# A hybrid decoder layer on one core: 32 more tokens take the gathered-rows path of the expert stage, 352 dense token columns instead of 384

## The chip, the cores and the metric

The kernel runs on one core of a Trainium2 chip. The metric is the device time of one execution in microseconds (us), lower is better. TensorE (PE) multiplies, VectorE (DVE) and ScalarE (ACT) work elementwise, GpSimd (POOL) issues the indirect DMAs, SyncE (SP) issues most other DMAs. 16 DMA engines serve all queues.

## What is computed

One decoder layer of 512 tokens with 2048 features in float32: two token mixers, a merge with a residual, an expert stage (PEER), a gated per-layer input and a last norm. The change touches the expert stage alone. It is, cut to what matters:

```python
q = (hf @ wq).reshape(N, PEER_HEADS, 2, half)            # 8 heads
s1 = jnp.einsum('nhc,kc->nhk', q[:, :, 0], k1)           # 128 keys per half
s2 = jnp.einsum('nhc,kc->nhk', q[:, :, 1], k2)
v1, i1 = lax.top_k(s1, 16); v2, i2 = lax.top_k(s2, 16)
cand = (v1[..., :, None] + v2[..., None, :]).reshape(N, PEER_HEADS, 256)
cv, ci = lax.top_k(cand, 16)
e_idx = i1[ci // 16] * 128 + i2[ci % 16]                 # one of 16384 experts
gate = softmax(cv)
z = einsum('thkd,td->thk', u_tab[e_idx], h)              # 128 slots per token
out = einsum('thk,thkd->td', gelu(z) * gate, v_tab[e_idx])
```

Each token has 128 slots (8 heads of 16 experts). A slot costs a dot product with a row of `u_tab` and an addition of a scaled row of `v_tab`, rows of 2048 float32 (8 KB).

## The kernel before

The features lie on the partitions and the tokens along the free axis, except where rows are gathered. Every float32 weight is used as a high and a low float32r part: `Stream.split` makes the high part on ACT (L111) and the low part on DVE (L112), and `mm3` (L147 to L149) does three matmuls per pair of tiles. The weights come through rings: four raw halves of 512 KB, four high and four low halves. `Ahead.step` loads two blocks ahead and splits one block ahead.

The 512 tokens of the expert stage are in two groups.

- **Group A**, the first 128 tokens (`NA`), takes the gathered-rows path. Its tokens are on the partitions. For slot s one indirect DMA (L779, on POOL's queue) fetches 128 rows of 8 KB, 1 MB together, one row for each token. `dot_u` multiplies them with the tokens' own rows `hrow` and sums (L785, DVE, 128x2048), for 128 slots. In the second half the same is done with `peer_v`: `axpy_v` adds each row times its coefficient to `outA` (L1083, DVE, 128x2048). There are two row buffers: each `dot_u` or `axpy_v` ends with the gather into the buffer that it has just read, so the gather for slot s+2 waits for the dot of slot s.
- **Group B**, the other 384 tokens (`NB`), takes the dense path: all 16384 experts. The loop over `j` (`NU` = 128 steps, "the U loop") multiplies 128 experts of `u` with the 384 columns `hBh`, `hBl`: 16 tiles of features times three matmuls, 48 matmuls of 384 columns a step. The result goes through Gelu to DRAM (`z_s`, L984 and L985). The gate matrix [i1, i2, token] is made by `gate_tokens`, four tokens (a quad) at a time: four one-hot rows on DVE (L833) and ACT (L832, L838), four matmuls of 256 columns (L843), and a copy and an addition into `stage` (L848 on ACT, L849 on DVE), which goes to `G_s` in DRAM. The loop over groups of eight blocks and 8 pairs of output tiles (`NV` = 120 steps, "the V loop", and 8 last steps) loads `z_s` and `G_s` again, multiplies them (L1003), splits (L154, L155), does 48 matmuls of 384 columns a step and adds the result up (L1091).

The order is written by hand (`manual_schedule`): an engine executes its instructions in the order in which the code emits them. In a step of the U loop stand on DVE: the two low parts of the next block, the additions into `stage` that were left over, then a share of a list `work` (the top-k of the three blocks of group B and the quads, each with a cost, 16 steps for the first block's top-k, 2 times 36 steps for top-k and quads together, 22 steps for the last quads), and then the dots. The dots are spread evenly over 120 steps (from step 7 on): 128 dots are one a step, and two in every 15th step. In a step of the V loop stand on DVE: two low parts, the second addition of the step before (L1091), the product of gate and activation (L1003), the axpys, spread over the 120 steps like the dots, the low part of the activation (L155), and the first addition (L1091), which waits for PE.

Two lines set the pace of dots and axpys:

```python
while dots and 129 - len(dots) <= 128 * n / (NU - 1 - NF) + 1e-9:     # U loop, NF = 7
while axpys and 129 - len(axpys) <= 128 * (n + 1) / NV + 1e-9:        # V loop
```

Of the kernel before, what the change touches and what calls it, by code (L numbers as in the profile page):

```python
# [10 lines left out]
F32 = mybir.dt.float32  # L11
F32R = mybir.dt.float32r
# [8 lines left out]
T = 512  # L21
D = 2048
KT = 16
NA = 128
NB = T - NA
NJ = 8
# [20 lines left out]
def kernel(ctx: ExitStack, tc: tile.TileContext, a, dbg=None):  # L47
# [14 lines left out]
    # ---------------------------------------------------------------- helpers  # L62
# [14 lines left out]
    class Ring:  # L77
        """Buffers taken in turn."""
# [42 lines left out]
    class Ahead:  # L121
        """Streams of a list of blocks: loaded two steps ahead, split one step ahead."""
# [28 lines left out]
    def split(hi, lo, src, gain=None):  # L151
        """hi + lo = src * gain, both float32r."""
# [29 lines left out]
    def rstd_cols(ss, n, name):  # L182
        """[128 tokens, blocks] of 1/sqrt(ss/n + eps)."""
# [13 lines left out]
    def sums_over_features(sq):  # L197
        """[128 tokens, 4] PSUM sums over the partitions of sq [128, T]."""
# [6 lines left out]
    def rows_of(rc, out=None):  # L205
        """[128, tokens], in out or else in PSUM: every partition holds the row of rc."""
# [11 lines left out]
    class SumSq:  # L218
        """Sum of squares of [128, T] chunks over features."""
# [18 lines left out]
    # ---------------------------------------------------------------- constants  # L238
# [21 lines left out]
    # ---------------------------------------------------------------- DRAM scratch  # L260
# [39 lines left out]
    # ---------------------------------------------------------------- HGRN2  # L300
# [147 lines left out]
    # ---------------------------------------------------------------- gates (kept before the sigmoid)  # L448
# [6 lines left out]
    # ---------------------------------------------------------------- MLA  # L455
# [17 lines left out]
    # rotary tables: angle = position * frequency, reduced to [-pi, pi]  # L473
# [49 lines left out]
    for hp in range(4):  # L523
# [21 lines left out]
        # a head's rotary part: its 64 rows of high parts, and in the other 64 rows their low parts  # L545
# [58 lines left out]
    # ---------------------------------------------------------------- merge  # L604
# [35 lines left out]
    # ---------------------------------------------------------------- residual, second norm  # L640
# [20 lines left out]
    hBl = hpool.tile([128, 16, NB], F32R, name="hBl")  # L661
    hrow = hpool.tile([128, D], F32, name="hrow")
# [38 lines left out]
    def topk(b, i1o, i2o, gate):  # L701
        """Steps (cost, function) that fill i1o, i2o, gate: [128 tokens, 8 heads * 16] float32."""
# [57 lines left out]
    # ---- group A: expert rows gathered for the first 128 tokens  # L760
    def prep_A():
# [3 lines left out]
        def experts():  # L765
            V.scalar_tensor_tensor(i1, i1, 128.0, i2, op0=OP.mult, op1=OP.add)
            V.tensor_copy(eA, i1)
            gather(a["peer_u"], 0)
            gather(a["peer_u"], 1)
# [5 lines left out]
    in_flight = {}  # L775

    def gather(tab, s):
        row = rows()
        G.indirect_dma_start(out=row, out_offset=None, in_=tab,  # L779
                             in_offset=bass.IndirectOffsetOnAxis(ap=eA[:, s:s + 1], axis=0))  # L780
        in_flight[s] = row

    def dot_u(s):
        row = in_flight.pop(s)
        V.scalar_tensor_tensor(row, row, 1.0, hrow, op0=OP.mult, op1=OP.mult,  # L785
                               accum_out=zA[:, s:s + 1])
        if s + 2 < 128:
            gather(a["peer_u"], s + 2)
        else:
            gather(a["peer_v"], s + 2 - 128)  # L790

    # ---- group B: the gate matrix [i1, i2, token]
# [3 lines left out]
    def prep_B(b):  # L796
        i1 = upool.tile([128, 128], F32, name="i1", bufs=2)
        i2 = upool.tile([128, 128], F32, name="i2", bufs=2)
        gt = upool.tile([128, 128], F32, name="gt", bufs=1)

# [16 lines left out]
        return topk(b + 1, i1, i2, gt) + [(0, turn)]  # L817
# [3 lines left out]
    def gate_tokens(t0):  # L821
        """Gate matrices of tokens t0 .. t0+3 of group B."""
# [35 lines left out]
    def merge(*lists):  # L858
        """The lists' steps in one list, each list spread evenly over it."""
# [10 lines left out]
    # ---------------------------------------------------------------- PEER scores  # L870
# [38 lines left out]
    def rows_of_h(c):  # L909
        """Group A's h by rows, 512 of its columns."""  # L910
# [7 lines left out]
        S.activation(hrow[:, c * 512:(c + 1) * 512], ps, AF.Copy)  # L918

    pending = None  # L920
    for cg in range(4):
# [28 lines left out]
        if cg == 0:  # L950
# [4 lines left out]
            zA = gpool.tile([128, 128], F32, name="zA")  # L955
            rows = Ring(gpool, 2, [128, D], F32, "row")
# [5 lines left out]
            # the top-k steps of group A that need the heads of a column group only  # L962
# [10 lines left out]
    hApool.release()  # L973

# [5 lines left out]
    dots = list(range(128))  # L980

    def finish(z, j):
        zg = t2()[:, :NB]
# [26 lines left out]
    for j in range(NU):  # L1010
# [6 lines left out]
        if j >= NF:  # L1017
# [14 lines left out]
        if j == 1:  # L1032
            scores_mul(3, pending)
        todo = after_pe + after_pe_next
# [6 lines left out]
        if j == NU - 7:  # L1041
# [6 lines left out]
            zts = Ring(vwA, 2, [128, 4, NB], F32, "zt")  # L1048
            gts = Ring(vwA, 2, [128, NB // TC, 4, TC], F32, "gt")
            vwB = tc.alloc_tile_pool(name="vwB", bufs=1, side="left")  # L1050
            ahs = Ring(vwB, NJ, [128, NB], F32R, "ah")
            als = Ring(vwB, NJ, [128, NB], F32R, "al")
# [9 lines left out]
    dump("zA", zA)  # L1062
    hpool.release()
# [3 lines left out]
    outA = V_.tile([128, D], F32, name="outA")  # L1067
# [308 lines left out]
```

## Time and profile before

| | |
|---|---|
| median of 3 runs | 4041.68 us (4041.59 to 4042.62) |
| span of the profiled execution, first to last instruction | 4040.0 us |
| PE busy | 4005.3 us, 99% |
| DVE busy | 2621.1 us, 65% |
| ACT busy | 1597.2 us, 40% |
| U loop, 128 steps | about 1643 to 2771 us of the span |
| V loop, 120 steps and 8 last ones | about 2771 to 3836 us |
| clock granted to PE | full in every stage but the last |

The page gives no other time of the profiled execution than its span; the median of the runs is 1.7 us longer. Busy times are averages over stages with different limits, so the section of rows below takes the stages one by one. Matmuls are pipelined, so the time that one costs is read from the distance of the starts of its neighbours, not from its duration. The same holds for DVE's instructions: each row's duration reaches a little into the next one's.

### The profile page before, as it was taken

The numbers are of one execution on the slowest core, as the hardware profiler recorded it, in microseconds if no ns is written. First come the engines' busy times: TensorE is split into PE (matmuls) and PEld (weight loads), VectorE is DVE, ScalarE is ACT, GpSimd is POOL, SyncE is SP. The second block draws the span as 40 slices with busy tenths as digits, with TensorE's granted clock in tenths as the row PEclk, the third lists the DMA queues.
The fourth block names the chain that finished last, engine by engine and source line by source line (L and its number), as shares of the span: only waits on it lengthen the run. The fifth ranks groups of instructions, "written<-read, shape, count | busy, mean of one in ns | idle before, by whom it ended". The sixth has DMA issues, their size and how long they took to land. (4 is left out here: it accounts for less than half of the span.)

```text
span 4040.0 us, 54629 instructions
## 1 busy us (share of the span) xinstructions
PE 4005.3 (99%) x21191; PEld 3667.2 (91%) x21191; DVE 2621.1 (65%) x3992; ACT 1597.2 (40%) x2582; POOL 347.6 (9%) x262
## 2 busy tenths in 40 slices
PE   9999999999999999999999999999999999999998
PEld 7878777778888889999999999999999999999976
DVE  5352554443343343699998998977777888877744
ACT  5342433332332242325566555753333333333443
POOL 0000000000000000021221211111111111111000
PEclk9999999999999999999999999999999999999999
DMA  5222222334444442478787788789888888888432
GB/s 210 97 74 94 72 96 84 102 105 141 151 141 133 141 140 99 166 286 304 283 303 283 287 302 298 293 332 356 317 297 315 312 311 312 299 313 310 169 117 97
DMA packets 264515, 862.68 MB, mean 214 GB/s; under 512 B 24128, under 2 KB 94272, under 8 KB 229568
## 3 DMA queue, kind: packets, MB, share of 16 engines
q1 hardware_dynamic: 202064, 531.57, 38.5%
q0 software_dynamic: 36864, 268.45, 17.8%
q10 hardware_dynamic: 25328, 59.17, 3.8%
q8 instruction: 168, 2.75, 0.3%
q14 instruction: 91, 0.75, 0.1%
HBM read 780.44 MB, written 78.64 MB: 213 GB/s over the span
## 5 line engine op out<-in xcount | busy, mean ns | idle before, releaser
L111 ACT ACTIVATE hi<-raw 128x1024 fp32r<-128x1024 f32 x806 | 851.4, 1059 | 1606.9 <-PE acc L148 1371.9
L112 DVE TENSOR_TENSOR lo<-raw,hi 128x1024 fp32r<-128x1024 f32 x806 | 975.0, 1221 | 782.6 <-ACT hi L111 779.5
L147 PE MATMUL acc<-hBh,hi 128*128 128x384 f32 x2304 | 775.0, 336 | 0.0
L148 PE MATMUL acc<-hBl,hi 128*128 128x384 f32 x2304 | 774.5, 336 | 0.0
L149 PE MATMUL acc<-hBh,lo 128*128 128x384 f32 x2304 | 774.4, 336 | 0.0
L148 PEld LDWEIGHTS acc<-hBl,hi 128*128 128x128 f32 x2304 | 433.1, 188 | 3.0 <-DVE hBl L155 0.2
L147 PEld LDWEIGHTS acc<-hBh,hi 128*128 128x128 f32 x2304 | 433.1, 188 | 2.7
L149 PEld LDWEIGHTS acc<-hBh,lo 128*128 128x128 f32 x2304 | 433.1, 188 | 0.0
L779 POOL DMA_INDIRECT row<-in_peer_u_dram,eA x128 | 198.9, 1554 | 2551.1 <-DMA raw<-in_uT_dram 1703.2
L149 PE MATMUL acc<-xh,lo 128*128 128x512 f32 x912 | 363.9, 399 | 0.0
L147 PE MATMUL acc<-xh,hi 128*128 128x512 f32 x912 | 363.4, 398 | 0.0
L148 PE MATMUL acc<-xl,hi 128*128 128x512 f32 x912 | 362.6, 398 | 0.0
L147 PE MATMUL acc<-ahx,hi 128*128 128x384 f32 x1024 | 344.7, 337 | 0.0
L148 PE MATMUL acc<-alx,hi 128*128 128x384 f32 x1024 | 344.1, 336 | 0.0
L149 PE MATMUL acc<-ahx,lo 128*128 128x384 f32 x1024 | 344.1, 336 | 0.0
L147 PE MATMUL acc<-ah,hi 128*128 128x384 f32 x1024 | 344.1, 336 | 0.0
L148 PE MATMUL acc<-al,hi 128*128 128x384 f32 x1024 | 344.1, 336 | 0.0
L149 PE MATMUL acc<-ah,lo 128*128 128x384 f32 x1024 | 344.1, 336 | 0.0
L1083 DVE SCALAR_TENSOR_TENSOR outA<-row,coef,outA 128x2048 f32<-128x2048 f32 x127 | 298.0, 2346 | 16.6 <-DMA row<-in_peer_v_dram,eA 16.3
L785 DVE SCALAR_TENSOR_TENSOR row<-row,hrow 128x2048 f32<-128x2048 f32 x128 | 292.0, 2283 | 20.5 <-DMA row<-in_peer_u_dram,eA 20.4
L779 POOL DMA_INDIRECT row<-in_peer_v_dram,eA x128 | 147.5, 1152 | 860.3 <-DVE outA L1083 799.6
L149 PEld LDWEIGHTS acc<-xh,lo 128*128 128x128 f32 x912 | 171.4, 188 | 43.0 <-issue 2.4
(379 smaller groups left out, 6270.5 us busy)
## 6 DMA issues: line engine op xcount, KB each, us to landing
raw<-in_uT_dram SPq DMA_DIRECT2D x256, 512.0 KB, 6.9
raw<-in_vB_dram SPq DMA_DIRECT2D x256, 512.0 KB, 5.7
z_s<-t ACTq DMA_DIRECT2D x128, 192.0 KB, 4.9
G_s<-stage ACTq DMA_DIRECT2D x12, 2048.0 KB, 14.4
zt<-z_s SPq DMA_DIRECT2D x32, 768.0 KB, 7.4
gt<-G_s SPq DMA_DIRECT2D x32, 768.0 KB, 12.1
raw<-in_w_ga_dram SPq DMA_DIRECT2D x32, 512.0 KB, 3.5
raw<-in_w_gb_dram SPq DMA_DIRECT2D x32, 512.0 KB, 3.5
```

The costliest lines, as they stand in the source:

```text
L111: S.activation(hi, raw, AF.Copy)
L112: V.tensor_tensor(lo, raw, hi.bitcast(F32), op=OP.subtract)
L147: TE.matmul(out, lhsT=lh, rhs=rh, start=start, stop=False)
L148: TE.matmul(out, lhsT=lh, rhs=rl, start=False, stop=False)
L149: TE.matmul(out, lhsT=ll, rhs=rh, start=False, stop=stop)
L779: G.indirect_dma_start(out=row, out_offset=None, in_=tab, in_offset=bass.IndirectOffsetOnAxis(ap=eA[:, s:s + 1], axis=0))
L785: V.scalar_tensor_tensor(row, row, 1.0, hrow, op0=OP.mult, op1=OP.mult, accum_out=zA[:, s:s + 1])
L1083: V.scalar_tensor_tensor(outA, row, coef[:, s:s + 1], outA, op0=OP.mult, op1=OP.add)
```

## The change

32 tokens (`NX`, the last of group B) leave the dense path. `ND` = 352 columns remain in it. The 32 tokens, called X, take the gathered-rows path: with four copies of each token on the 128 partitions, partition r*32+t holds part r of token t's slots, so 32 gathers of 1 MB (and not 128) hold its 128 slots. `dot_u` and `axpy_v` run over 160 row sets in place of 128, in the same number of steps: one, one, two, and so on. The U rows of X come last, the V rows of X first. New are `rows_of_hX` (X's rows, four copies, in U steps 2 to 5), `experts_X` (indices and gates moved to the four parts), an accumulator `outX`, and in the last 8 steps two more transposes each and the sum of the four parts. The top-k of the third block of group B, which holds X, is now made first, and its quads, 24 instead of 32, come first too. The projection that makes the scores still has 384 columns.

```diff
+NX = 32
+RX = 128 // NX
 NB = T - NA
+ND = NB - NX
...
-    z_s = dram.tile([128 // NJ, 128, NJ, NB], F32, name="z_s")
-    G_s = dram.tile([NB // TC, 128, 128 * TC], F32, name="G_s")
+    z_s = dram.tile([128 // NJ, 128, NJ, ND], F32, name="z_s")
+    G_s = dram.tile([ND // TC, 128, 128 * TC], F32, name="G_s")
...
+    hBd = [(hBh[:, k, :ND], hBl[:, k, :ND]) for k in range(16)]
...
-    in_flight = {}
...
-    def dot_u(s):
-        row = in_flight.pop(s)
-        V.scalar_tensor_tensor(row, row, 1.0, hrow, op0=OP.mult, op1=OP.mult,
-                               accum_out=zA[:, s:s + 1])
...
+    in_flight = []
+    order = [(a["peer_u"], 0, s) for s in range(128)] + [(a["peer_u"], 1, s) for s in range(NX)]
+    order += [(a["peer_v"], 1, s) for s in range(NX)] + [(a["peer_v"], 0, s) for s in range(128)]
...
+    def dot_u():
+        row, x, s = in_flight.pop(0)
+        z = zX if x else zA
+        V.scalar_tensor_tensor(row, row, 1.0, hrowX if x else hrow, op0=OP.mult, op1=OP.mult,
+                               accum_out=z[:, s:s + 1])
+        gather()
...
+        def experts_X():
+            e, x = t2()[:, :128], slice(128 - NX, 128)
+            V.scalar_tensor_tensor(e[x], i1[x], 128.0, i2[x], op0=OP.mult, op1=OP.add)
+            for r in range(RX):
+                V.tensor_copy(eX[r * NX:(r + 1) * NX], e[x, r * NX:(r + 1) * NX])
+                S.activation(gateX[r * NX:(r + 1) * NX], gt[x, r * NX:(r + 1) * NX], AF.Copy)
...
-    quads = [[(2, lambda t=t: gate_tokens(t)) for t in range(b * 128, (b + 1) * 128, 4)] for b in range(3)]
+    quads = [[(2, lambda t=t: gate_tokens(t)) for t in range(b * 128, min((b + 1) * 128, ND), 4)] for b in range(3)]
...
-            work = phase(B0, prep_B(0))
-            for b in (1, 2):
-                prep = prep_B(b)
-                work += phase(MIX, merge(prep[:-1], quads[b - 1]) + prep[-1:])
-            work += phase(NW - NF - B0 - 2 * MIX, quads[2])
+            work = phase(B0, prep_B(2))
+            for b, b1 in ((2, 0), (0, 1)):
+                prep = prep_B(b1)
+                work += phase(MIX, merge(prep[:-1], quads[b]) + prep[-1:])
+            work += phase(NW - NF - B0 - 2 * MIX, quads[1])
...
-            while dots and 129 - len(dots) <= 128 * n / (NU - 1 - NF) + 1e-9:
-                dot_u(dots.pop(0))
-        z = acc()[:, :NB]
+            while dots and NDOT + 1 - dots <= NDOT * n / (NU - 1 - NF) + 1e-9:
+                dots -= 1
+                dot_u()
+        z = acc()[:, :ND]
         for k in range(KT):
-            mm3(z, *cur.part(k, KT), hBh[:, k], hBl[:, k], k == 0, k == KT - 1)
+            mm3(z, *cur.part(k, KT), *hBd[k], k == 0, k == KT - 1)
...
+        if 2 <= j < 6:
+            rows_of_hX(j - 2)
...
-            while axpys and 129 - len(axpys) <= 128 * (n + 1) / NV + 1e-9:
-                axpy_v(axpys.pop(0))
+            while axpys and NDOT + 1 - axpys <= NDOT * (n + 1) / NV + 1e-9:
+                axpys -= 1
+                axpy_v()
...
+            V.tensor_reduce(sX[h], oT[:, h * 256 + 128:h * 256 + 256].rearrange("p (r t) -> p t r", r=RX),
+                            axis=AX.X, op=OP.add)
+            V.tensor_tensor(x2[:, d, NA + ND:], x2[:, d, NA + ND:], sX[h], op=OP.add)
```

How the order changes is shown at two places. The first is DVE in the U loop, late in the stretch of top-k and quads. `row` is a row buffer, `lo` the low part of a weight block, `ohr` a quad's one-hot rows, `stage` the gate matrix, `zA` the dots' results; the rows of the scratch tile `t` (L738 to L741, after the change L742 to L745) look up indices. Before:

```order
L785 SCALAR_TENSOR_TENSOR row_9654,zA<-row_9654,hrow 128x2048
L112 TENSOR_TENSOR lo_80<-raw_72,hi_76 128x1024
L112 TENSOR_TENSOR lo_81<-raw_73,hi_77 128x1024
L833 SCALAR_TENSOR_TENSOR ohr<-cst,slots 128x256 x8
L785 SCALAR_TENSOR_TENSOR row_9653,zA<-row_9653,hrow 128x2048
L112 TENSOR_TENSOR lo_82<-raw_74,hi_78 128x1024
L112 TENSOR_TENSOR lo_83<-raw_75,hi_79 128x1024
```

And after the change, at a step with two dots:

```order
L796 SCALAR_TENSOR_TENSOR row_9657,zA<-row_9657,hrow 128x2048
L115 TENSOR_TENSOR lo_80<-raw_72,hi_76 128x1024
L115 TENSOR_TENSOR lo_81<-raw_73,hi_77 128x1024
L848 SCALAR_TENSOR_TENSOR ohr<-cst,slots 128x256 x8
L796 SCALAR_TENSOR_TENSOR row_9656,zA<-row_9656,hrow 128x2048
L796 SCALAR_TENSOR_TENSOR row_9657,zA<-row_9657,hrow 128x2048
L115 TENSOR_TENSOR lo_82<-raw_74,hi_78 128x1024
L115 TENSOR_TENSOR lo_83<-raw_75,hi_79 128x1024
```

The second of two dots in a step reads the buffer that the last dot of the step before had read (`row_9657` here); this now happens in every third step, before in every 15th.

The second place is DVE in the V loop; `zt` is the gated activation, `al` its low part, `x` the accumulator of the dense tokens, `acc` PSUM. Before:

```order
L112 TENSOR_TENSOR lo_82<-raw_74,hi_78 128x1024
L112 TENSOR_TENSOR lo_83<-raw_75,hi_79 128x1024
L1091 TENSOR_TENSOR x_21808<-x_21808,acc 128x384
L1003 TENSOR_TENSOR zt_21390<-zt_21390,gt_21392 128x384
L1083 SCALAR_TENSOR_TENSOR outA<-row_9654,coef,outA 128x2048
L155 TENSOR_TENSOR alx_21828<-zt_21390,ahx_21820 128x384
L1091 TENSOR_TENSOR x_21808<-x_21808,acc 128x384
```

And after the change, in a step with two axpys:

```order
L115 TENSOR_TENSOR lo_80<-raw_72,hi_76 128x1024
L115 TENSOR_TENSOR lo_81<-raw_73,hi_77 128x1024
L1133 TENSOR_TENSOR x_21705<-x_21705,acc 128x352
L1037 TENSOR_TENSOR zt_21282<-zt_21282,gt_21284 128x352
L1124 SCALAR_TENSOR_TENSOR outA<-row_9656,coef,outA 128x2048
L1124 SCALAR_TENSOR_TENSOR outA<-row_9657,coef,outA 128x2048
L158 TENSOR_TENSOR al_21299<-zt_21282,ah_21291 128x352
L1133 TENSOR_TENSOR x_21705<-x_21705,acc 128x352
```

The four small operations have 352 columns, and every third step has a second axpy ahead of the low part and the addition that PE waits for.

## Rows read from the trace of the kernel before

**Rows 1.** The page: busy times of the engines, and DVE in 40 slices.

```profile
PE 4005.3 (99%) x21191; PEld 3667.2 (91%) x21191; DVE 2621.1 (65%) x3992; ACT 1597.2 (40%) x2582; POOL 347.6 (9%) x262
...
DVE  5352554443343343699998998977777888877744
```

**Rows 2.** Windows by stage: start:end, length, busy PE PEld DVE ACT POOL, clock, DMA share, GB/s.

```profile
1651.65:1705.68 54.03, 54.03 (x324) 54.03 (x323) 41.62 (x98) 20.05 (x25) 0.79 (x1) 1.00 0.46 155
1705.68:1838.80 133.12, 133.12 (x770) 133.12 (x769) 127.34 (x299) 42.90 (x51) 29.38 (x19) 1.00 0.82 297
1838.80:2154.37 315.57, 314.33 (x1850) 313.50 (x1849) 291.03 (x540) 184.46 (x401) 63.13 (x39) 1.00 0.80 294
2154.37:2481.08 326.71, 321.13 (x1860) 316.63 (x1860) 292.27 (x541) 185.68 (x403) 58.68 (x39) 1.00 0.79 289
2481.08:2679.45 198.37, 198.37 (x1186) 198.34 (x1186) 174.28 (x250) 145.89 (x357) 35.22 (x24) 1.00 0.83 308
2679.45:2771.14 91.69, 91.69 (x531) 91.69 (x531) 60.78 (x64) 30.31 (x43) 15.82 (x12) 1.00 0.96 353
2771.14:3769.54 998.40, 998.40 (x5762) 998.40 (x5761) 795.27 (x848) 318.65 (x364) 143.40 (x126) 1.00 0.87 310
3769.54:3836.10 66.56, 66.56 (x390) 66.33 (x389) 47.86 (x74) 32.07 (x43) 0.00 (x0) 1.00 0.41 135
```

**Rows 3.** Timeline of PE in the U loop: start, duration, instruction.

```profile
2599.75 0.34 PE L149 MATMUL acc<-hBh,lo 128*128 128x384 f32 x1
...
2604.95 0.34 PE L149 MATMUL acc<-hBh,lo 128*128 128x384 f32 x1
2605.13 1.11 PE L843 MATMUL wide<-ohr,ohl 128*128 128x256 f32 x8
2606.07 0.34 PE L147 MATMUL acc<-hBh,hi 128*128 128x384 f32 x1
```

**Rows 4.** Timeline of DVE in the U loop, where nothing waits.

```profile
2607.68 1.28 DVE L849 TENSOR_TENSOR stage<-stage,wide 128x512 f32<-128x512 f32 x2 [0.21 <-ACT stage L848]
2608.88 3.25 DVE L833 SCALAR_TENSOR_TENSOR ohr<-cst,slots 128x256 fp32r<-128x256 f32 x8
2612.05 2.28 DVE L785 SCALAR_TENSOR_TENSOR row<-row,hrow 128x2048 f32<-128x2048 f32 x1
...
2614.26 2.50 DVE L112 TENSOR_TENSOR lo<-raw,hi 128x1024 fp32r<-128x1024 f32 x2
```

**Rows 5.** Timeline of DVE in the U loop at a step with two dots.

```profile
2221.45 2.28 DVE L785 SCALAR_TENSOR_TENSOR row<-row,hrow 128x2048 f32<-128x2048 f32 x1
...
2227.13 2.28 DVE L785 SCALAR_TENSOR_TENSOR row<-row,hrow 128x2048 f32<-128x2048 f32 x1
...
2232.74 2.29 DVE L785 SCALAR_TENSOR_TENSOR row<-row,hrow 128x2048 f32<-128x2048 f32 x1 [3.32 <-DMA row<-in_peer_u_dram,eA]
```

**Rows 6.** Timeline of DVE in the V loop, at two axpys and at one.

```profile
3265.06 2.35 DVE L1083 SCALAR_TENSOR_TENSOR outA<-row,coef,outA 128x2048 f32<-128x2048 f32 x1
3269.86 2.35 DVE L1083 SCALAR_TENSOR_TENSOR outA<-row,coef,outA 128x2048 f32<-128x2048 f32 x1 [2.46 <-DMA row<-in_peer_v_dram,eA]
...
3276.27 2.34 DVE L1083 SCALAR_TENSOR_TENSOR outA<-row,coef,outA 128x2048 f32<-128x2048 f32 x1
3278.53 0.55 DVE L155 TENSOR_TENSOR al<-zt,ah 128x384 fp32r<-128x384 f32 x1
```

**Rows 7.** The gathers, 1706 to 2679 us: who waited (us, times), issue to landing.

```profile
  DVE row L785: 19.5, 10
...
DMA to landing us min/median/max: 5.8/9.0/14.1
```

**Rows 8.** The same of the V loop, 2776 to 3769 us.

```profile
  DVE outA L1083: 16.3, 7
...
DMA to landing us min/median/max: 5.4/6.6/11.5
```

**Rows 9.** The same of the U loop's end, 2680 to 2771 us.

```profile
DMA to landing us min/median/max: 5.5/9.7/12.6
```

**Rows 10.** DMA queues, 2900 to 3740 us: the gathers' packets, MB, share of 16 engines.

```profile
q0 software_dynamic: 15603, 113.56, 37.3%
```

More of the change, by code (lines that the diff above doesn't have):

```diff
@@ L767, in experts @@
             V.tensor_copy(eA, i1)
-            gather(a["peer_u"], 0)
-            gather(a["peer_u"], 1)
+            gather()
+            gather()
             dump("eA", eA)
@@ L773, in prep_A, with gather @@
         return topk(0, i1, i2, gateA) + [(1, experts)]
-    in_flight = {}
[L777 to L781, printed above, removed]
-    def dot_u(s):
-        row = in_flight.pop(s)
-        V.scalar_tensor_tensor(row, row, 1.0, hrow, op0=OP.mult, op1=OP.mult,
-                               accum_out=zA[:, s:s + 1])
[L787 to L790, printed above, removed]
+    in_flight = []
+    order = [(a["peer_u"], 0, s) for s in range(128)] + [(a["peer_u"], 1, s) for s in range(NX)]
+    order += [(a["peer_v"], 1, s) for s in range(NX)] + [(a["peer_v"], 0, s) for s in range(128)]
+    def gather():
+        if order:
+            tab, x, s = order.pop(0)
+            row = rows()
+            e = eX if x else eA
+            G.indirect_dma_start(out=row, out_offset=None, in_=tab,
+                                 in_offset=bass.IndirectOffsetOnAxis(ap=e[:, s:s + 1], axis=0))
+            in_flight.append((row, x, s))
+    def dot_u():
[3 more added lines that the diff above has]
+                               accum_out=z[:, s:s + 1])
+        gather()
     slots = {}
@@ L815, in turn @@
             hold[0] = 2
-        return topk(b + 1, i1, i2, gt) + [(0, turn)]
+        return topk(b + 1, i1, i2, gt) + ([(0.5, experts_X)] if b == 2 else []) + [(0, turn)]
     stage = [None]
@@ L918, in rows_of_h, with rows_of_hX @@
         S.activation(hrow[:, c * 512:(c + 1) * 512], ps, AF.Copy)
+    def rows_of_hX(c):
+        o = slice(c * 4, c * 4 + 4)
+        t = t2()
+        t4 = t.rearrange("p (k r t) -> p k r t", k=4, r=RX)
+        V.tensor_tensor(t4, hBh[:, o, None, ND:].bitcast(F32).to_broadcast([128, 4, RX, NX]),
+                        hBl[:, o, None, ND:].bitcast(F32).to_broadcast([128, 4, RX, NX]), op=OP.add)
+        ps = mx()
+        for k in range(4):
+            s = slice(k * 128, k * 128 + 128)
+            TE.transpose(ps[:, s], t[:, s], ident)
+        S.activation(hrowX[:, c * 512:(c + 1) * 512], ps, AF.Copy)
     pending = None
@@ L979 @@
     start_up = {2: by_group[3], 3: rest[:4], 4: rest[4:7], 5: rest[7:9], 6: rest[9:]}
-    dots = list(range(128))
+    NDOT = 128 + NX
+    dots = NDOT
     def finish(z, j):
-        zg = t2()[:, :NB]
+        zg = t2()[:, :ND]
         S.activation(zg, z, AF.Gelu)
@@ L1073, with axpy_v @@
         r.tiles = [r.tiles[(r.at + i) % NJ] for i in range(NJ)]
-        r.tiles = r.tiles + [vwC.tile([128, NB], F32R, name=f"{name}x{i}") for i in range(NJ)]
+        r.tiles = r.tiles + [vwC.tile([128, ND], F32R, name=f"{name}x{i}") for i in range(NJ)]
         r.at = NJ
     assert len(aT) == NJ
-    def axpy_v(s):
-        row = in_flight.pop(s)
+    def axpy_v():
+        row, x, s = in_flight.pop(0)
+        o, c = (outX, coefX) if x else (outA, coef)
         if s == 0:
-            V.tensor_scalar(outA, row, coef[:, 0:1], None, op0=OP.mult)
+            V.tensor_scalar(o, row, c[:, 0:1], None, op0=OP.mult)
         else:
-            V.scalar_tensor_tensor(outA, row, coef[:, s:s + 1], outA, op0=OP.mult, op1=OP.add)
-        if s + 2 < 128:
-            gather(a["peer_v"], s + 2)
+            V.scalar_tensor_tensor(o, row, c[:, s:s + 1], o, op0=OP.mult, op1=OP.add)
+        gather()
+    S.activation(coefX, zX, AF.Gelu)
+    V.tensor_tensor(coefX, coefX, gateX, op=OP.mult)
     S.activation(coef, zA, AF.Gelu)
@@ L1099 @@
     late = []
-    axpys = list(range(128))
+    axpys = NDOT
     NV = (NGRP - 1) * 8
@@ L1136, in finish_x2 @@
         ds = (dp * 2, dp * 2 + 1)
+        sX = [tmp.tile([128, NX], F32, name="sX", bufs=2) for _ in ds]
         for h, d in enumerate(ds):
             add_up(ps[h], d)
-            V.tensor_tensor(x2[:, d, :NA], x2[:, d, :NA], oT[:, h * 128:h * 128 + 128], op=OP.add)
+            V.tensor_tensor(x2[:, d, :NA], x2[:, d, :NA], oT[:, h * 256:h * 256 + 128], op=OP.add)
+            V.tensor_reduce(sX[h], oT[:, h * 256 + 128:h * 256 + 256].rearrange("p (r t) -> p t r", r=RX),
+                            axis=AX.X, op=OP.add)
+            V.tensor_tensor(x2[:, d, NA + ND:], x2[:, d, NA + ND:], sX[h], op=OP.add)
         for d in ds:
@@ L1157 @@
             d = dp * 2 + half
-            TE.transpose(oT[:, half * 128:half * 128 + 128], outA[:, d * 128:(d + 1) * 128], ident)
+            for i, o in enumerate((outA, outX)):
+                TE.transpose(oT[:, half * 256 + i * 128:half * 256 + i * 128 + 128], o[:, d * 128:(d + 1) * 128], ident)
         late.append(lambda dp=dp, ps=ps, oT=oT: finish_x2(dp, ps, oT))
```

20 lines of the change are left out of this document (14 added, 6 removed).

## Prediction

> **What bounds the kernel now.** I read the page first, then the windows by stage, then the timelines of PE and DVE inside the two loops, then who waits for the gathers. On the page PE is busy 99% of the span and DVE 65%, which says "PE, nothing else"; but DVE's slices stand at 9 through the U loop [rows 1]. The windows tell why the average misleads. I call steps 7 to 22, 23 to 58, 59 to 94 and 95 to 116 of the U loop (the second to fifth window) its middle: 110 steps, 973.8 us, DVE busy 127.3 + 291.0 + 292.3 + 174.3 = 884.9 us, that is 91%. In the V loop DVE is busy 795 of 998 us, 80%, and the DMA engines' share is 0.87 [rows 2].
>
> PE's price of a step comes from the starts of neighbours. Thirty spacings of 384-column matmuls take 5.20 us, 173.3 ns each, so 48 take 8.32 us; eight of 256 columns take 0.94 us, 117.5 ns each [rows 3]. Over the middle that is 110 x 8.32 plus 96 quads x 0.47 = 960 us of the 974. In the V loop 120 x 8.32 = 998.4 is the whole window. So PE is the bound in both loops, with DVE 9% and 20% below it.
>
> **Fewer columns.** Between 256 and 384 columns a matmul's spacing grows by 55.8 ns, 0.436 ns a column. 32 columns less are 14.0 ns, a step falls from 8.32 to 7.65 us: 0.67 us. The 256-column row also says that loading new weights each time does not hold the spacing above 117.5 ns. If PE alone counted, 12,288 matmuls (256 steps of 48) would give back 171 us.
>
> **What DVE gets, U loop.** Every count here is of the middle.
> - Dots: 146 in place of 117, each 2.21 us from start to the next start [rows 4]: 29 x 2.21 = +64.1.
> - Quads: 88 in place of 96. A quad is four one-hot rows of 3.17/8 = 0.396 us and one addition of 1.20/2 = 0.60 us [rows 4], 2.19 us: 8 x 2.19 = -17.5.
> - `experts_X`: five DVE operations on 32 partitions. The trace has none; between 0 and five times the 0.55 us of a 384-column operation [rows 6], 2.8; I take 1.0, because they have at most 128 columns. ACT's four copies lie in its idle time (57% busy here) [rows 2].
>
> 884.9 + 64.1 - 17.5 + 1.0 = 932.5 us of DVE work. PE's would be 110 x 7.65 + 88 x 0.47 = 883. **DVE becomes the bound of the middle**, by 50 us, even before it waits for anything.
>
> **What it waits for.** There are two row buffers, and a gather starts when the dot that read the buffer ends. In a step with two dots, the second one reads the buffer that the dot of the step before released. Between lies one step's other DVE work and one dot: (884.9 - 117 x 2.21)/110 = 5.7 us, less 0.2 for the fewer quads, plus 2.2: 7.7 us. A gather takes 9.0 us in the median from issue to landing [rows 7]. So the second dot comes too early by 1.3 us at the median. That is the low end. Such a step: the dot that starts at 2221.45 releases the buffer, and the second dot of the next pair waits 3.32 us for it [rows 5]; that is the high end. In all, the middle has 19.5 us of such waits [rows 7] on 7 steps with two dots, 2.8 each, with one or two that belong to other dots; I take 2.6. So far this cost little, since DVE had slack; where DVE is the bound, each wait counts in full. The change makes such steps 36 in the middle (every third): 36 x 2.6 = 94 us, between 47 and 120. Middle: 932.5 + 94 = 1026, that is **+52 us** (+6 to +78).
>
> The ends of the U loop stay with PE. Six steps up to 1705.68 [rows 2]: -4.0, and 16 transposes of `rows_of_hX` at no more than a 256-column spacing, 0 to 1.9, taken as 1: **-3 us**; its four additions lie in 12 us of DVE's idle time. Eleven last steps: -7.4 us, and DVE (60.8 us of 91.7, plus some four dots and as many waits) fits; but the DMA share is 0.96 there, so the low gain is 0. I take **-7 us**.
>
> **V loop.** DVE: 795.3 + 32 axpys x 2.26 us (3276.27 to 3278.53 [rows 6]) = +72.3; 480 small operations lose 32 of 384 columns, at most a twelfth of 0.55 us each, 22 us; I take 16, since some of each is fixed. 851.6 us, against PE's 918. The wait at a step with two axpys: the other work of a step is 4.1 us, plus one axpy 6.4; the gather's median is 6.6 us [rows 8], so 0.2 us is the low end; measured are 16.3 us on 8 such steps, 2.0 each. But latency depends on load. A gather costs the 16 engines 0.373 x 840/108.3 = 2.9 us (108.3 gathers of 1.049 MB in 113.56 MB [rows 10]). 32 more add 93 us to 0.87 x 998 = 869; less some 10 for the smaller `zt` and `gt`, that is 951 us, more than PE's 918. The engines would be full, and the row nearest to that is the U loop's end, share 0.96, where the median is 9.7 us [rows 9]: a wait of 3.3. I take 3.0, near that end: 40 x 3.0 = 120. 851.6 + 120 = 972, **-27 us**; the ends are PE's 918 (-80) and 851.6 + 40 x 3.3 = 984 (-15).
>
> The Trainium skill ("DMA: Bandwidth & Descriptors", section Specifications) puts what one core gets of HBM at about 358 GB/s. Estimated by that page, the V loop could not go below 948 us (310 GB/s x 8.32 us plus 0.25 MB more a step, 2.83 MB, is 7.90 us a step), so its low end would be -50 and not -80; the highest rate in the rows of stages here, 353 GB/s, agrees.
>
> The eight last steps: 8 x 0.67 = **-5 us**; DVE is busy 47.9 of 66.6 us there, and two sums and two additions of 32 columns a step fit.
>
> **Sum.** -3 + 52 - 7 - 27 - 5 = +10 us. The span was 4040.0; the runs' median, 1.7 us above it, is what I predict from: 4041.7 + 10 = **4052 us**. The saving of PE is spent on DVE's dots and on rows that come late.
>
> **Rivals.**
> - *The rows come in time.* If the wait per pair of dots is at its median value, 1.3 us, the middle costs +6, and the V loop comes down to the DMA engines' 951 us (-47): -3 + 6 - 7 - 47 - 5 = -56, **3986 us**, faster. It decides at 1.15 us a pair, where the middle costs nothing. For it: the quickest gathers land after 5.8 us, inside the 7.7 [rows 7]. Against it: the mean wait is 2.8, and gathers get more company, not less.
> - *Late rows feed on each other.* Waits at the high ends: +78 in the middle, -15 in V, nothing at the U loop's end: -3 + 78 + 0 - 15 - 5 = +55, **4097 us**.
> - *The columns do not set the spacing*, so that the change does not do what it says on PE: 173 ns stay. The middle is DVE's anyway (+52), the rest gives nothing: **4094 us**. The 256-column row speaks against it.
> - *DVE keeps up everywhere*: -171, **3870 us**. Against it stands the sum of 932 against 883.
> - *PE idles enough to lose its clock.* PE would be busy 883 of 1026 us in the middle. If in one step in ten its clock fell to the lower level, 1.2 in place of 2.4 GHz, 48 x 2 x 0.159 = 15.3 us in place of 9.3 for 11 steps are +65: **4117 us**. In the window that ends at 2481.08 PE lost 5.6 us and its clock stayed at 1.00 [rows 2], which speaks against it. The Trainium skill ("TensorE: Matmul & The Clock Gate", section on the clock gate) says that a PE that sits idle is put back to half its clock; no row of the stages here shows that.
>
> **How the numbers follow.** Chances: forecast (4030 to 4085) 0.46, rows in time 0.30, late rows 0.14, spacing 0.03, DVE keeps up 0.03, clock 0.04. A measurement here tells some 0.2%, 8 us, from no change. Faster by more: 0.26 of "in time", 0.03 and 0.02 of the forecast's low side, 0.31. Within: 0.04 and 0.14, 0.18. Slower: 0.30 + 0.14 + 0.03 + 0.04 = 0.51. The range takes in the forecast, most of "in time" and most of "late rows": 3975 to 4105. The forecast's own is 4030 to 4085.
>
> **What would show it.** Right: in the middle DVE at 90% or more of every window, and the rest of its time waits for rows; PE with gaps, steps of about 9.3 us; U-loop matmuls 159 ns apart at the loop's end; waits for rows near 90 us in the U loop and 120 in V; V steps of 8.1 us at a DMA share of 0.95 or more; the clock at 1.00. Wrong: a middle under 974 us, V steps at 7.65 us, a spacing that did not fall, or a wait for something else than rows.

## The result and the profile after

The changed kernel takes **4104.7 us** (median of 4 runs, 4102.9 to 4110.8) against 4041.6 us: a ratio of 1.0157, 95% interval [1.0143, 1.0172]. It is slower by 63 us, where 10 were forecast. The sign is right; the size is outside the forecast's own 4030 to 4085, inside the range.

DVE in the 40 slices of the page of the changed kernel; [rows 1] has the same of before:

```profile
PE 3946.5 (96%) x21191; PEld 3577.5 (87%) x21191; DVE 2729.5 (67%) x4090; ACT 1555.7 (38%) x2519; POOL 439.3 (11%) x326
DVE  5342554433343344799888988887888888888844
```

PE's busy time fell by only 59 us and it now has gaps, and DVE is not filled in the U loop either: 8 where 9 stood. Neither engine is busy enough to be the bound by itself. The windows by stage of the changed kernel (columns as in [rows 2]):

```profile
1650.80:1719.10 68.30, 56.04 (x341) 55.01 (x340) 44.85 (x102) 21.46 (x30) 2.02 (x2) 0.93 0.39 133
1719.10:1866.70 147.60, 134.96 (x799) 132.94 (x798) 136.71 (x310) 43.29 (x55) 34.77 (x21) 0.95 0.81 291
1866.70:2197.70 331.00, 302.58 (x1783) 293.75 (x1781) 291.61 (x519) 161.93 (x328) 73.14 (x48) 0.94 0.83 298
2197.70:2546.30 348.60, 319.84 (x1860) 307.68 (x1859) 313.18 (x563) 184.76 (x402) 79.95 (x48) 0.96 0.81 300
2546.30:2758.90 212.60, 202.52 (x1189) 195.90 (x1188) 184.64 (x263) 145.22 (x357) 47.71 (x29) 0.94 0.85 315
2758.90:2856.30 97.40, 91.13 (x543) 89.64 (x544) 67.40 (x69) 29.54 (x42) 22.17 (x15) 0.96 0.95 355
2856.30:3834.40 978.10, 949.70 (x5751) 944.93 (x5750) 846.69 (x881) 299.92 (x366) 178.37 (x158) 0.99 0.95 348
3834.40:3899.90 65.50, 65.50 (x415) 65.32 (x414) 53.39 (x103) 32.27 (x43) 0.00 (x0) 1.00 0.41 137
```

The head (steps 1 to 6) grew from 54.0 to 68.3 us, the middle from 973.8 to 1039.8, the U loop's tail (eleven steps) from 91.7 to 97.4. For the last two stages I use one pair of edges in both kernels, the end of the last axpy and the first matmul of the stage behind; by these the kernel before has 997.9 and 68.7 us (two us from [rows 2] in all), so V gave back 19.8 and the last eight steps 3.2. Sum: +14.3 + 66.0 + 5.7 - 19.8 - 3.2 = +63.

What DVE waits for in the middle, and then in the V loop, from the view of waits (us, times, longest):

```profile
DVE row L796 <- DMA row<-in_peer_u_dram,eA: 92.4, 34, 7.3
DVE lo L115 <- ACT hi L114: 8.5, 7, 2.6
DVE row L796 <- DMA row<-in_peer_u_dram,eX: 6.8, 2, 6.3
...
DVE outA L1124 <- DMA row<-in_peer_v_dram,eA: 94.5, 39, 5.7
DVE outX L1124 <- DMA row<-in_peer_v_dram,eX: 21.7, 10, 3.6
DVE zt L1037 <- DMA gt<-G_s: 7.1, 7, 2.0
```

Row waits were 19.5 and 16.3 us before [rows 7, 8]; they are 99.2 and 116.2.

The head has a fault of its own. DVE, then PE, then ACT in U step 3, from their timelines (start, duration, instruction, idle time before it and its releaser):

```profile
1664.88 0.48 DVE L696 MAX8 val<-scores 128x8 f32<-128x128 f32 x2
...
1673.89 0.68 DVE L940 TENSOR_TENSOR t<-hBh,hBl 128x512 f32<-128x512 f32 x1
1677.41 2.36 DVE L115 TENSOR_TENSOR lo<-raw,hi 128x1024 fp32r<-128x1024 f32 x2 [2.84 <-ACT hi L114]
```

```profile
1674.71 1.09 PE L945 MATMUL wide<-cst,t 128*128 128x128 f32 x4 [6.77 <-DVE t L940]
...
1676.19 0.49 PE L152 MATMUL acc<-hBh,lo 128*128 128x352 f32 x1
1676.48 0.49 PE L150 MATMUL acc<-hBh,hi 128*128 128x352 f32 x1
...
1679.88 0.32 PE L150 MATMUL acc<-hBh,hi 128*128 128x352 f32 x1
1680.04 0.32 PE L151 MATMUL acc<-hBl,hi 128*128 128x352 f32 x1
```

```profile
1675.84 0.60 ACT L946 ACTIVATE hrowX<-wide 128x512 f32<-128x512 f32 x1 [11.97 <-PE wide L945]
1676.33 2.00 ACT L114 ACTIVATE hi<-raw 128x1024 fp32r<-128x1024 f32 x2
```

The addition of `rows_of_hX` (L940) stands behind 9 us of top-k on DVE. PE's transposes (L945) wait 6.77 us for it, ACT's copy (L946) for the transposes, and the next block's high parts stand behind that copy. The next step starts late, and PE comes out of the gap at half clock: spacing 0.29 us, then 0.16.

### The profile page after: what moved, and what is told of

Same layout as the page of the kernel before. It is cut to its first block, busy times and chain, and to the rows that moved or that the text cites. A ratio compares the mean times of both kernels' runs of the same rounds, so it can differ in the third digit from the quotient of the medians.

```text
span 4102.4 us, 54793 instructions
## 1 busy us (share of the span) xinstructions
PE 3946.5 (96%) x21191; PEld 3577.5 (87%) x21191; DVE 2729.5 (67%) x4090; ACT 1555.7 (38%) x2519; POOL 439.3 (11%) x326
## 5 line engine op out<-in xcount | busy, mean ns | idle before, releaser
L152 PE MATMUL acc<-hBh,lo 128*128 128x352 f32 (+1 forms) x2304 | 761.9, 331 | 20.1 <-DVE lo L115 20.1
L151 PE MATMUL acc<-hBl,hi 128*128 128x352 f32 (+1 forms) x2304 | 761.3, 330 | 0.0
L150 PE MATMUL acc<-hBh,hi 128*128 128x352 f32 (+1 forms) x2304 | 760.4, 330 | 0.0
L151 PE MATMUL acc<-al,hi 128*128 128x352 f32 x1024 | 333.5, 326 | 16.3 <-DVE al L158 16.3
L151 PE MATMUL acc<-alx,hi 128*128 128x352 f32 x1024 | 332.7, 325 | 9.7 <-DVE alx L158 9.7
L150 PE MATMUL acc<-ah,hi 128*128 128x352 f32 x1024 | 336.8, 329 | 1.4 <-ACT hi L114 1.4
L150 PE MATMUL acc<-ahx,hi 128*128 128x352 f32 x1024 | 336.6, 329 | 0.5 <-DVE x L1133 0.5
L152 PE MATMUL acc<-ah,lo 128*128 128x352 f32 x1024 | 335.9, 328 | 1.2 <-DVE lo L115 1.2
L152 PE MATMUL acc<-ahx,lo 128*128 128x352 f32 x1024 | 335.5, 328 | 1.4 <-DVE lo L115 1.4
L151 PEld LDWEIGHTS acc<-al,hi 128*128 128x128 f32 x1024 | 194.9, 190 | 17.8 <-DVE al L158 17.8
```

The source lines that it names most:

```text
L150: TE.matmul(out, lhsT=lh, rhs=rh, start=start, stop=False)
L151: TE.matmul(out, lhsT=lh, rhs=rl, start=False, stop=False)
L152: TE.matmul(out, lhsT=ll, rhs=rh, start=False, stop=stop)
```

## The experiments

Times of whole runs are medians, ratios are against the kernel before, measured beside each run (4041.6 to 4043.4 us); the one time that rests on a single execution is called so. Windows and waits are read from one execution of each run. Executions of the kernels with two buffers and X's rows differ by up to 19 us (4072.3 to 4091.5 with both edits), so small differences between their windows say little.

**X's rows out of line (head).** `rows_of_hX` is now the addition alone and stands ahead of the top-k; `turn_hX` has the transposes, and the copy is among the things that ACT does in the step after:

```diff
+        if 2 <= j < 6:
+            tX = rows_of_hX(j - 2)
         for _, f in start_up.get(j, ()):
             f()
...
-            rows_of_hX(j - 2)
+            turn_hX(j - 2, tX)
...
-        S.activation(hrowX[:, c * 512:(c + 1) * 512], ps, AF.Copy)
+        late.append(lambda: S.activation(hrowX[:, c * 512:(c + 1) * 512], ps, AF.Copy))
```

> rows_of_hX in three parts: X's additions on VectorE first in the step, the transposes behind the step's matmuls as now, the copies on ScalarE behind the splits of the next step. Theory (in the changed kernel TensorE waits in U steps 2 to 5 for additions that stand behind 9 us of top-k, and ScalarE splits the next weights only behind the copy): the stretch from the end of U step 0 to that of step 6 falls from 68.3 us to about 51, total about 4087 (4082 to 4092). Rival (the top-k of group A alone is too long for the shorter steps, the additions only show it): the stretch stays above 62, total 4098 or more.

4090.3 us, ratio 1.0113 [1.0079, 1.0147]. The head's window:

```profile
1650.40:1706.90 56.50, 52.53 (x341) 51.73 (x340) 44.52 (x102) 22.41 (x30) 1.10 (x2) 1.00 0.45 148
```

The head is 56.5 us in place of 68.3: 12 of its 14 us came from the place of these few instructions in the order, and the clock stays full.

**X's expert output left out.** 352 columns, but group A's 128 row sets alone; `rows_of_hX`, `experts_X` and X's dots and axpys are left out, and so the output lacks X's expert part:

```diff
-    NDOT = 128 + NX
+    NDOT = 128
...
-        if 2 <= j < 6:
-            rows_of_hX(j - 2)
```

> 352 dense columns, but no gathered rows for the 32 tokens: their expert output is left out (128 row sets in each half, as before the change). It prices the columns alone. Theory (TensorE's spacing falls with the columns, VectorE has room without the 32 row sets): about 165 us less than the kernel before, 3875 (3865 to 3895). Rival (VectorE or the DMA engines hold the middle of the U loop even without the 32 row sets): 3920 or more.

A single execution: 3921.7 us, where 3875 was expected. Middle and V loop:

```profile
1703.20:2632.90 929.70, 908.14 (x5621) 895.15 (x5620) 863.48 (x1589) 531.69 (x1136) 192.79 (x118) 0.99 0.83 305
...
2719.50:3651.80 932.30, 932.30 (x5749) 932.30 (x5748) 780.75 (x849) 313.54 (x364) 139.23 (x126) 1.00 0.90 329
```

The narrower columns are worth 120 us, not the 171 of "if PE alone counted", for two reasons. In the V loop PE is never idle, and its 5749 matmuls take 932.3 us: 0.162 us each, 7.8 us a step where the forecast had 7.65, so PE's floor there is 932 us and not 918. The middle, 929.7 us, is 66 us over DVE's busy time and 47 over the 883 that the working has for PE; of this, DVE waits 31.7 us for high parts of weights and still 23.5 for rows. X costs the rest: 4104.7 - 3921.7 = 183 us for 32 row sets twice and the head, where DVE's dots and axpys of X are busy for 72.9 and 72.8 us.

**384 columns on PE again**, results of 352 used:

```diff
+        zw = acc()
+        z = zw[:, :ND]
...
-            mm3(z, *cur.part(k, KT), *hBd[k], k == 0, k == KT - 1)
+            mm3(zw[:, :NB], *cur.part(k, KT), hBh[:, k], hBl[:, k], k == 0, k == KT - 1)
```

> The changed kernel with its U-loop matmuls at 384 columns again (the 32 extra columns are computed and not used). Theory (VectorE's work and its waits for rows set the U loop's middle, TensorE does not, even though its clock is granted at 0.94 to 0.96 there): the middle stays at 1040 us within 12, only the loop's two ends grow by some 6 us, total about 4110 (4100 to 4125). Rival (TensorE with its lowered clock sets the middle): the middle grows by 74 us or more, total 4180.

4114.0 us, ratio 1.0170 [1.0142, 1.0198], which takes in the changed kernel's. The middle:

```profile
1720.50:2762.50 1042.00, 1005.31 (x5629) 984.15 (x5628) 927.85 (x1652) 535.68 (x1140) 234.46 (x145) 0.97 0.81 301
```

45 us more of busy PE, and a middle of 1042.0 against 1039.8. (The profiled execution was this run's fastest, 4101.3 us.) PE does not set the middle; its clock at 0.94 to 0.96 there takes from an engine that has time to spare.

**Dots and axpys spread in the step**, so that two of them no longer follow each other (the same is done with the axpys):

```diff
+            if due == 2:
+                dot_u()
...
             while work and spent < n and not hold[0] and len(after_pe) < 2:
                 c, f = work.pop(0)
                 f()
...
+                done += 1
+                if due == 1 and done == 1:
+                    dot_u()
+                    due = 0
+            if due:
                 dot_u()
```

> The changed kernel with the same 160 row sets in the same steps, but spread inside the steps: where a step has two, one stands ahead of the step's other VectorE work and one behind it, and a single one stands in the middle of it. Theory (VectorE waits for rows because two of them stand next to each other and the second one's buffer was released only some 7 us before): waits for rows fall from 123 to under 45 us in the U loop and from 116 to under 60 us in the V loop, the middle to about 965 us, total about 3985 (3955 to 4030). Rival (the DMA engines cannot bring 32 more row sets in the time, wherever they stand): the waits stay within a third of what they were, total 4080 or more.

4092.6 us, ratio 1.0115 [1.0085, 1.0145]: 12 us less, where the theory wanted about 120. Of the V loop, its window, who waited for rows, and a wait that is new:

```profile
2854.50:3833.30 978.80, 950.52 (x5775) 942.10 (x5774) 851.56 (x883) 292.75 (x364) 198.23 (x158) 1.00 0.94 347
...
  DVE outA L1134: 72.9, 33
  DVE outX L1134: 16.9, 10
...
DVE alx L158 <- ACT ahx L157: 11.8, 21, 0.6
DVE al L158 <- ACT ah L157: 10.7, 19, 0.6
```

The row waits shrink from 116 to 90 us, and the window does not get shorter. Its end, the last axpy, moved with the edit; from PE's first matmul of the loop to its first transpose behind it the loop takes 986.6 us against 990.2, 4 us less. The edit itself gives back most of the gain: in a step with two axpys none stands any longer between the product `zt` and its low part, so DVE waits in 40 steps for ACT's high part, 22.5 us in all, where it waited 0.6. The middle of the U loop is alike: 74.7 us of row waits in place of 99.2, but 25.6 for high parts of weights in place of 8.5, and 1037.3 us in place of 1039.8. My picture, a second row that comes just too early because it stands too near, was too small. What was left: the two buffers cannot go round faster, or the DMA engines, at a share of 0.94, bring no more, or the waits only change place.

**Both edits together, two buffers.**

> Two row buffers as in the changed kernel, with both earlier edits together: X's head work apart (15 us less alone) and the dot products spread in the step (12 us less alone). Theory: the two act at different places and add, 4105 - 15 - 12 = 4078 us, with row waits about as in the spread run (96 us in U, 90 in V). Rival (with the head in order the rows start earlier and feed the middle better): under 4065 us.

4081.5 us, ratio 1.0089 [1.0073, 1.0106]: near the sum of the two, and still slower than the kernel before. With two buffers no order of these instructions that was tried gets below it.

**Three row buffers**, with X's rows out of line. To make room, the quads' one-hot tiles lie where group A's hidden state was, and one tile of an earlier stage (`rr_mix`) lies in another pool:

```diff
-            rows = Ring(gpool, 2, [128, D], F32, "row")
+            rows = Ring(gpool, 3, [128, D], F32, "row")
...
             gather()
             gather()
+            gather()
```

> The changed kernel with X's head work apart (as in the earlier run that gave 4090.3 us) and three row buffers in place of two, so that three gathers are under way; to make room, the one-hot tiles of the gate matrix lie where group A's hidden state was. Theory (the loop of two buffers): a buffer goes round in about 10 us from issue to landing and 2.2 us of dot product, so two buffers give a row every 6.1 us and three one every 4.1 us; the V loop needs one every 5.8 us and DVE's own work in the middle of the U loop one every 5.8 us. Row waits fall below 40 us in U and 30 in V, the middle of the U loop goes from 1036 to about 945 us, the V loop from 978 to about 935, and the whole to about 3950 us. Rival (the DMA engines give no more): issue to landing grows from about 10 to about 15 us, V stays over 970 and the middle over 1020, and the whole is 4080 to 4095 us. Second rival (the waits only change place: DVE gets its rows but stands for PE): row waits fall, and the middle and V stay over 1010 and 965.

**3988.2 us**, ratio 0.9868 [0.9851, 0.9884]: 102 us under the same kernel with two buffers, and faster than the kernel before. Head, the four windows of the middle, tail, V and the last eight steps:

```profile
1650.90:1707.30 56.40, 52.54 (x342) 51.74 (x341) 44.55 (x102) 22.41 (x31) 1.08 (x1) 1.00 0.45 150
1707.30:1849.10 141.80, 132.63 (x799) 130.43 (x799) 136.36 (x310) 43.31 (x55) 42.99 (x23) 0.98 0.85 311
1849.10:2145.20 296.10, 290.25 (x1788) 286.17 (x1787) 292.83 (x519) 161.38 (x328) 95.30 (x48) 0.99 0.89 335
2145.20:2470.70 325.50, 312.60 (x1861) 301.94 (x1860) 311.93 (x562) 184.42 (x403) 92.68 (x48) 0.98 0.85 321
2470.70:2668.70 198.00, 193.65 (x1185) 188.88 (x1183) 183.64 (x263) 144.20 (x356) 54.39 (x29) 0.98 0.89 340
2668.70:2763.00 94.30, 90.84 (x550) 89.38 (x550) 67.61 (x69) 29.70 (x43) 25.99 (x15) 0.98 0.97 367
2763.00:3716.70 953.70, 941.96 (x5761) 939.63 (x5761) 849.34 (x881) 306.74 (x366) 257.71 (x157) 1.00 0.94 356
3716.70:3781.20 64.50, 64.04 (x395) 63.86 (x395) 53.22 (x103) 31.61 (x42) 0.00 (x0) 0.97 0.40 139
```

The middle is 961.4 us for 924.8 of DVE work, 96%; PE is busy for 97% too, at a clock of 0.98. That DVE's work sets it, as the working had it, is borne out by the two runs on the tail's rows below. How long a gather takes in the middle from issue to landing (min, median, max), after the change and with three buffers, and who still waits for rows:

```profile
DMA to landing us min/median/max: 5.5/8.6/14.3
```

```profile
  DVE row L797: 8.3, 2
...
DMA to landing us min/median/max: 5.7/9.0/14.4
```

The gathers did not become quicker (in the V loop the median went from 7.7 to 8.6 us), the row waits fell from 99.2 to 8.3 us and in the V loop from 116.2 to none, and the engines carry more (327 against 301 GB/s over the middle). The rows were late because a third gather could not be issued, not because the DMA engines were full. The rival that they give no more falls. The size was overrated: 3950 us, a middle of 945 and a V loop of 935 were expected. DVE's other waits in the V loop tell what is late next:

```profile
DVE lo L115 <- ACT hi L114: 54.7, 45, 2.5
DVE zt L1042 <- DMA gt<-G_s: 45.5, 14, 6.3
```

The gates `gt`, 7 us of waits with two buffers, are 45 with three. That they keep V at 954 and not 932 is read from the trace, not tested.

**Three buffers and the spreading.**

> As the run with three row buffers and X's head work apart, and the dot products and axpys of a step spread among its other DVE work instead of in one block behind it. Theory (the loop of two buffers was the limit): with a third buffer a block of two dot products finds its rows landed anyway, so the order within a step moves the whole by less than 10 us, to about 3945 us. Rival (what counts is how far rows stand apart): a further 15 us or more below the run without the spreading.

3991.0 us, ratio 0.9878 [0.9862, 0.9895]: no different in all. The middle and the V loop:

```profile
1707.00:2677.00 970.00, 926.00 (x5612) 901.75 (x5611) 925.80 (x1648) 534.09 (x1139) 206.93 (x148) 0.99 0.87 325
...
2772.80:3716.60 943.80, 939.54 (x5744) 937.59 (x5744) 849.84 (x882) 306.48 (x365) 223.71 (x157) 1.00 0.96 359
```

The whole does not move, as the theory had it, but two stages do, against each other: the middle is 9 us longer and the V loop 10 shorter. That the place in a step does not matter holds of their sum alone.

**The control: the kernel before with three buffers.**

> The kernel before with three row buffers in place of two and nothing else in its arithmetic: the control. Theory (a row every 6.1 us from two buffers is enough for 128 rows, one every 7.6 us): the 36 us of row waits that the kernel before has in the middle of U and in V go, but PE and DVE there wait for each other, so 4020 to 4042 us. Rival (three gathers under way slow the weight transfers): slower than 4050 us.

4034.8 us, ratio 0.9980 [0.9970, 0.9990]. Its row waits are gone (0.5 us in both loops) and that is worth 8 us, since PE bounds it. So neither the third buffer nor the tiles moved for it explain the 102 us alone; they are worth that to a kernel whose DVE has no slack. Against this control the 32 tokens on gathered rows, with the head in order, gain 4034.8 - 3988.2 = 47 us; with two buffers and the same head they lost 47 (4090.3 against 4043.2).

**The tail's rows.** All dots done by step 115, then, in a second run, the opposite, two in each of the last eleven steps (both with three buffers and the head in order):

```diff
-            while dots and NDOT + 1 - dots <= NDOT * n / (NU - 1 - NF) + 1e-9:
+            while dots and NDOT + 1 - dots <= NDOT * n / (NU - 12 - NF) + 1e-9:
...
+            while dots and NDOT + 1 - dots <= 138 * min(n, 109) / 109 + 2 * max(0, n - 109) + 1e-9:
```

> Three row buffers and X's head work apart (that run: 3988 us; middle of the U loop 961 us, the eleven steps of its tail 94.3 us at 367 GB/s, 1.02 times the 92 us of the kernel before although each has 32 columns less), with the U loop's 160 dot products all done by step 115: none in the tail. Theory (the tail is set by the bytes that the DMA engines bring there: weights, 13 rows, the first activations): 13 MB fewer, so the tail falls to PE's 352-column pace, 85 to 88 us; the middle carries 13 dots more (30 us of DVE) and grows to 980 to 992, the whole to about 4008 us. Rival (the tail is set by ACT and DVE standing for the first group's activations, not by bytes): the tail stays over 92 us.

> As the run with three row buffers and X's head work apart, but each of the last eleven steps of the U loop does two dot products and the steps before fewer: 7 dots (15 us of DVE) leave the middle for the tail. Theory (the tail is set by bytes, 7 MB more at 370 GB/s): middle 945 to 950 us, tail 108 to 113, the whole within 5 us of 3988. Rival (the tail has room, only DVE's work in the middle counts): tail under 98 us and the whole about 3975 us.

4010.4 us (0.9915 [0.9899, 0.9932]) and 3995.1 us (0.9880 [0.9863, 0.9896]). The tails:

```profile
2704.60:2790.10 85.50, 85.42 (x533) 85.15 (x533) 36.08 (x42) 29.91 (x43) 0.00 (x0) 1.00 0.71 251
```

```profile
2655.30:2771.50 116.20, 96.04 (x551) 92.81 (x551) 83.42 (x84) 29.53 (x42) 40.72 (x22) 0.94 0.96 365
```

Without rows the eleven steps run at PE's pace; with the 15 gathers of the even spread they take 94.3 us at 367 GB/s, with 22 116.2 at 365 (expected 108 to 113). The tail is set by bytes, as the theory had it, and what it gains the middle loses: 997.6 us for 956.6 of DVE work in the first run (expected 980 to 992), 948.3 for 910.7 in the second. With the 961.4 for 924.8 of the even spread that is 37 to 41 us over DVE's work each time, with the same matmuls on PE: the middle goes with DVE's work. The gathers go with the dots, so bytes are not told apart from it, but the DMA share is 0.86 or 0.87 in all three. In the tail of the changed kernel the dots wait 23.7 us for rows, where DVE has slack, and ACT waits for weights; ACT in the changed kernel and in the one before:

```profile
ACT hi L114 <- DMA raw<-in_uT_dram: 34.6, 10, 7.2
```

```profile
ACT hi L111 <- DMA raw<-in_uT_dram: 3.3, 1, 3.3
```

## Why the prediction was too low

| | forecast | measured | three buffers |
|---|---|---|---|
| head | -3 | +14.3 | +2.4 |
| middle of the U loop | +52 | +66.0 | -12.4 |
| tail of the U loop | -7 | +5.7 | +2.6 |
| V loop | -27 | -19.8 | -44.2 |
| last eight steps | -5 | -3.2 | -4.2 |
| sum | +10 | +63 | -56 |

(The last column sets the run with three buffers and X's rows out of line against the kernel before.)

**What held.** The columns: matmuls of 352 stand 0.16 us apart in the U loop, where 0.159 was forecast, and a tail without rows takes 85.5 us for 533 of them. (In the V loop they are 0.162, so the 171 us for PE alone were too many, but little of that is in the sum.) DVE's work: 926.1 us in the middle (932.5 forecast), 846.7 in V (851.6). The row waits: 99.2 and 116.2 us (94 and 120). The mechanism, that PE's saving is eaten by DVE's dots and by rows that come late, is what the runs show: undo either half, by leaving X out or by a third buffer, and the kernel is faster than before. Of the signs that the prediction named, two did not come: DVE is at 93, 88, 90 and 87% of the middle's four windows and not at 90 in each, and the clock is not at 1.00.

**What failed** are four steps, in order of size.

1. *Head*, 17 us: "its four additions lie in 12 us of DVE's idle time". A sum of idle time says nothing of where in the order an instruction stands. L940 stood behind the top-k, and two engines queued behind L940. The run with these out of line gave 12 back.
2. *Middle*, 14 us: DVE's work and row waits were taken for the whole. They are 926.1 + 99.2 = 1025.3 of 1039.8; high parts of weights that come late are 8.5 more, and 6 us are other small idle times. The forecast's own 932.5 + 94 = 1026 came out, with 6 us less work and 5 more of row waits; what it put at nothing are these other waits, 14.5 us. Mechanism right, size short.
3. *Tail*, 13 us: its low end was "no gain", since the DMA share was 0.96. It needed the bytes counted: 355 GB/s over 97.4 us are 34.6 MB, 2.2 more than the 353 over 91.7 of before [rows 2], and at 353 GB/s these take 98 us. At a full share more bytes are a loss, not a gain that fails to come.
4. *V and the last steps*, 9 us: 846.7 + 116.2 make 962.9 of 978.1; the gates and high parts of weights (7.1 and 5.9) were not in the sum.

Together 53 us, the whole difference.

**Where the sum was luckier than the reasoning.** The forecast priced a wait per pair of dots or axpys, and the totals came out, in the V loop by luck. By DVE's timeline the second dot of a step waits 82.4 of the middle's 99.2 us, 2.3 a pair (2.6 forecast). In the V loop the second axpy of a step waits only 74.3 of 116.2, 1.9 a pair (3.0 forecast), and 41.9 us stand at the first or only axpy of a step, which the forecast had at nothing. The rows of before say so too: of the 16.3 us of row waits in the V loop [rows 8] only the 2.46 of [rows 6] stand at a second axpy; the other six waits are at a step's first, so "2.0 each" for a step with two was misread. The 3.0 came from gathers that land in 9.7 us at a high DMA share; at the share of 0.95 the V loop's landed in 7.7 in the median. And with the pairs apart most waits stayed: what is short is the ring of buffers. One round of a buffer in the V loop of the changed kernel, on POOL and on DVE:

```profile
3300.19 0.94 POOL L789 DMA_INDIRECT row<-in_peer_v_dram,eA  x1 [5.29 <-DVE outA L1124]
...
3310.97 0.98 POOL L789 DMA_INDIRECT row<-in_peer_v_dram,eA  x1 [6.69 <-DVE outA L1124]
```

```profile
3300.68 2.35 DVE L1124 SCALAR_TENSOR_TENSOR outA<-row,coef,outA 128x2048 f32<-128x2048 f32 x1 [0.76 <-DMA row<-in_peer_v_dram,eA]
...
3308.35 2.35 DVE L1124 SCALAR_TENSOR_TENSOR outA<-row,coef,outA 128x2048 f32<-128x2048 f32 x1 [1.32 <-DMA row<-in_peer_v_dram,eA]
```

The gather issued at 3300.19 is what the axpy at 3308.35 waits for, and the next gather into its buffer is issued at 3310.97: 10.8 us a round, so two buffers give a row every 5.4 us. PE's step of 7.8 us (932.3 us by 120 steps, in the run without X), with four rows in three steps, wants one every 5.8. That margin of 0.4 us cannot make good a late landing, and landings spread over 5.3 to 11.6 us in the V loop and 5.5 to 14.3 in the middle. Three buffers would give one every 3.6 us, an estimate from the same round. How the spread turns into just these waits was not taken apart.

**The rivals.** *The rows come in time* gave 3986 us as -56; the kernel with a third buffer, where they do come in time, takes 3988.2. That the two are so near is luck: the terms differ by up to 18 us. With two buffers the case did not arise. *Late rows feed on each other*, 4097 us, is the nearest to the result, but it has no loss in the head and the tail. *PE loses its clock* was given 0.04 for want of a row: the granted clock did fall, to 0.94 to 0.96 in the U loop. It was back at 0.98 and 0.99 when rows came in time; the run with 384 columns says that the middle did not hang on it. *The columns do not set the spacing* falls with 0.16 us for 0.173, and *DVE keeps up everywhere*, 3870 us, was not reached even without X's rows (3921.7).

The Trainium skill ("DMA: Bandwidth & Descriptors", section Specifications) gave about 358 GB/s to a core, and V no less than 948 us by it. The runs go past it: the tail with three buffers moved 367 GB/s, and V with three buffers and the spreading took 943.8 us at 359.

## What to carry to other kernels

Before moving work onto gathered rows, work out how often the ring of buffers can hand one over, (issue to landing + use + issue) / buffers, and compare it with how often the loop wants one; where the margin is smaller than the spread of the landings, pay for another buffer first. Idle time of an engine hides an added instruction only if the instruction's place in the order lies in it: look at what stands ahead of it and who is queued behind its reader. Where the DMA share is near 1, price a stage by its bytes.

## What the runs showed of the hardware that I had not expected

PE lost its full clock inside a loop that keeps it busy otherwise: behind the head's 6.77 us without work its 352-column matmuls stood 0.29 us apart in place of 0.16, the lower of its two levels, 1.2 in place of 2.4 GHz. The Trainium skill ("TensorE: Matmul & The Clock Gate", section on the clock gate) says that an idle PE is put back to half; these rows agree.

A share of 0.94 to 0.95 of the DMA engines was no full house: with three gathers under way V went from 348 to 356 GB/s at such a share, the median landing there from 7.7 to 8.6 us, and in the middle only from 8.6 to 9.0.
